# Last two experts' downs at the end of the load order, first two experts gathered as one pair, one stream of modulation weights later in the order: one layer of a GLA, MLA and MoE block on one core

## The chip, the core and the metric

One Trainium2 chip, one of its cores. The metric is the device time of one execution of the kernel in microseconds (us), as a median over runs. The core has five engines that run side by side, each with its own instruction stream: TensorE (PE in the profile, its weight loads PEld), VectorE (DVE), ScalarE (ACT), GpSimd (POOL) and SyncE (SP), which here only issues DMA transfers. PEq, DVEq, ACTq and SPq are the parts of these engines that handle branches, waits and issues.

## What is computed

One layer over 256 tokens of width 1024. A mixer (gated linear attention beside latent attention, merged and projected) is added to the stream, then a MoE of 32 experts with four of them per token. Both are modulated by six vectors that come from one product of the conditioning with `w_mod`, 1024 x 6144. The MoE, cut to its core:

```python
def _moe(h, p):
    logits = (tok @ p["router_w"] + p["router_b"]).astype(jnp.float32)
    top_v, top_i = lax.top_k(logits, TOP_K)                  # 4 of 32
    wts = jax.nn.softmax(top_v, axis=-1)
    combine = jnp.sum(jax.nn.one_hot(top_i, N_EXPERTS) * wts[..., None], axis=1)
    for e in range(N_EXPERTS):
        gate = jnp.minimum(tok @ p["w_gate"][e] + p["b_gate"][e], SWIGLU_LIMIT)
        up = jnp.clip(tok @ p["w_up"][e] + p["b_up"][e], -SWIGLU_LIMIT, SWIGLU_LIMIT)
        act = (up + 1.0) * gate * jax.nn.sigmoid(SWIGLU_ALPHA * gate)
        out = out + combine[:, e:e + 1] * (act @ p["w_down"][e] + p["b_down"][e])
```

Each of an expert's three matrices is 1024 x 1024 in 32-bit floats. The result is x + gt_f * rmsnorm(out), over the last axis.

## The kernel before

**Before the experts.** In the first 300 us the kernel computes the modulation vectors, the mixer and the router. Its instructions stand in an order written out by hand (`tc.manual_schedule`), on every engine. Two strands of work are interleaved there: the projection of the hidden states by `w_in` (the products `p_gate<-h0h,wsl` and their like, fed by `split`, in which ACT rounds a block of weights to `wsh`, L370, and DVE takes the remainder `wsl`, L371; a call `Q(n)` puts the next n steps of it into the order) and the linear attention (`scores` gives the masked product `at` on DVE, L988; `inner` and `outer` sum `po` on TensorE; `normed_o` gives `on` on DVE, L1016; `outputs` turns it). The weights of modulation stream `g` come in four loads of 2 MB, g0 to g3, through two buffers; DVE adds each up in four instructions, two pairs of 128 x 1024 (L325). A string such as `"g2:0"` given to `Q` puts one pair there; `ring.done("g2")` behind the second pair frees the buffer, into which g3 is loaded.

**The expert weights.** They go through a ring of ten tiles of 2 MB (class `Ring`): an expert takes six, two each of w_gate, w_up and w_down, in this order. SyncE issues their loads (L76), in the order of the list `src`; the load into a tile is issued once the tile's last reader is done and `ring.done(n)` has stood in the program, n tiles at a time. The last up and the last down are cut into four pieces a tile; the last down is cut by columns (`w_down_last`), so that its left half of the output can be finished before its right half is loaded.

**One expert.** `select` (DVE, tensors `G`) marks the rows, up to 64, that are routed to it; `gather` multiplies them out of `x1` on TensorE (`p_xg`, two groups, g = 0 and 1) for a pair of experts at a time (EB = 2), and DVE and ACT modulate the outcome to `X` (L1344, L1367). `gather_one` does the same for one expert, with rows and columns the other way round and a turning (`p_xT`) behind; it is used for experts 0 and 1. `project` runs gate and up (`p_gate`, `p_up`; a first product with `selb` adds the bias), 32 passes each; `turn` turns the 64 rows of `u` to `aT`; `down` gives `p_y`, 32 passes; `halves` splits it into `yh` and `yl` (ACT and DVE); `scatter` adds these with S, which holds positions and weights (from `slot_tokens`, `p_st`), to `acc`, one expert later, ahead of the next down. So TensorE's order in expert e is: gate, up, a group of the gather for the next pair, `turn`, scatter of expert e-1, `p_st`, down.

**More than 64 rows.** `trips` holds, for each expert, a count that says whether another 32 rows are needed. The engines read it (`blocks`: `TENSOR_LOAD trips`, L1582) and branch: a body under `tc.If(rv > 0)` repeats gate, up and down for these rows. In this input it is entered in expert 0 and in one other. Expert 0 has such a branch behind each half of each matrix; experts 1 to 9 behind the gate (L1660), behind the up (L1666) and behind the down (L1726); experts 10 to 30 behind the up, with both projections in one body, and behind the down; expert 31 behind each half of the down (L1733). A branch with freed tiles behind it is followed by a new load of the count on SyncE, which stands behind the issue of the loads (`freed`).

**The end.** Behind expert 31, `acc` is squared and summed by columns (ACT, L1763, `jf`), normed, multiplied and added to `x1`, and stored.

The releases of expert 1 and later, as they stand:

```python
            if early:
                with tc.If(rv > 0):
                    X1, S1, g1 = more_first()
                rv = freed(2)
```

## Time and profile before

| | before |
|---|---|
| median of three runs | 1265.72 us (1265.17 to 1267.21) |
| the profiled execution | 1266.84 us |
| its span, first to last instruction | 1265.1 us |
| mean granted TensorE clock | 0.984 |
| TensorE busy | 1148.6 us (91%) |
| VectorE, ScalarE, GpSimd busy | 405.5, 246.6, 79.6 us |
| moved by DMA | 463.51 MB, 366 GB/s over the span |

A share of busy time is a mean over stages with different limits: in the first 300 us the DMA moves 104 to 364 GB/s a slice, and from 380 us on, but for one slice of 329 and the last, 410 to 428. The times of single instructions come from the profiled execution, so they add up to its span and not to the median; it lies 1.1 us above the median. Between the span and its time there are 1.7 us.

### The profile page before, as it was taken

The page shows a single profiled execution, that of the slowest core. Times are in us where ns is not written, and L with a number is a line of the kernel's source. Part 1 is how long each engine was busy: PE and PEld are TensorE (multiplying, and loading weights), DVE is VectorE, ACT ScalarE, POOL GpSimd, SP SyncE. Part 2 cuts the span into 40 slices and gives each one's busy share as a digit, 9 for nine tenths or more (in the row PEclk, how much of TensorE's full clock was granted, in tenths as well). Part 3 has the DMA queues.
Part 4 walks back from the last instruction along what each step waited for, and adds up shares of the span by engine and source line. Part 5 has one row for each costly group of instructions (what it writes and reads, how often), then busy time and mean ns, then how long its engine had stood idle before and what let it go on. Part 6 is the DMA issues. An engine that isn't in the chain of part 4 may idle for free. (4 is left out here: it accounts for less than half of the span.)

```text
span 1265.1 us, 16274 instructions
## 1 busy us (share of the span) xinstructions
PE 1148.6 (91%) x6484; PEld 603.1 (48%) x6487; DVE 405.5 (32%) x787; ACT 246.6 (19%) x432; POOL 79.6 (6%) x62
## 2 busy tenths in 40 slices
PE   8999989999999999999998899999879879999884
PEld 5776778885344444444443344444333333444321
DVE  5667676665321212212121222221111211122112
ACT  4566443452210010101010011010100100101001
POOL 2346001300000000000000000000000000000000
PEclk9999998999999999999999999999989999999998
DMA  9842545885789999999999999999799999999993
GB/s 364 328 180 104 225 179 219 338 338 235 306 352 410 425 424 426 425 427 425 425 427 426 425 428 426 425 425 427 329 413 427 425 426 426 426 427 425 426 413 127
DMA packets 38053, 463.51 MB, mean 366 GB/s; under 512 B 4600, under 2 KB 4856, under 8 KB 10400
## 3 DMA queue, kind: packets, MB, share of 16 engines
q1 hardware_dynamic: 37488, 461.42, 87.6%
q8 instruction: 100, 1.64, 0.5%
q14 instruction: 33, 0.27, 0.1%
q10 hardware_dynamic: 432, 0.18, 0.1%
HBM read 460.53 MB, written 1.05 MB: 365 GB/s over the span
## 5 line engine op out<-in xcount | busy, mean ns | idle before, releaser
L204 PE MATMUL p_up<-w,X 128*64 128x512 f32 x1024 | 229.4, 594 | 13.5 <-DMA w<-in_w_up_dram 11.2
L204 PE MATMUL p_y<-w,aT 128*64 128x512 f32 (+1 forms) x1088 | 236.4, 599 | 1.0 <-ACT aT L1482 1.0
L204 PE MATMUL p_gate<-w,X 128*64 128x512 f32 x1024 | 231.8, 601 | 3.1 <-DMA w<-in_w_gate_dram 2.7
L204 PEld LDWEIGHTS p_up<-w,X 128*64 128x64 f32 x1024 | 87.9, 137 | 140.1 <-issue 110.5
L204 PEld LDWEIGHTS p_gate<-w,X 128*64 128x64 f32 x1024 | 94.6, 138 | 117.0 <-issue 112.5
L204 PEld LDWEIGHTS p_y<-w,aT 128*64 128x64 f32 (+1 forms) x1088 | 72.5, 136 | 144.2 <-issue 140.7
L1505 DVE TENSOR_TENSOR yl<-p_y,yh 128x512 fp32r<-128x512 f32 x33 | 22.8, 691 | 227.9 <-ACT yh L1504 221.1
L1449 DVE TENSOR_SCALAR g<-p_gate 128x512 f32<-128x512 f32 x32 | 22.1, 692 | 221.1 <-PE p_gate L204 212.8
L204 PE MATMUL p_xg<-G,x 128*128 128x128 f32 x480 | 63.1, 284 | 24.1 <-PEq L1666 21.5
L204 PEld LDWEIGHTS p_xg<-G,x 128*128 128x128 f32 x480 | 57.5, 195 | 49.1 <-issue 49.0
L1482 ACT COPY aT<-p_aT 128x512 f32<-128x512 f32 (+1 forms) x34 | 19.5, 574 | 304.8 <-PE p_aT L1480 304.8
L1454 DVE TENSOR_SCALAR u<-p_up 128x512 f32<-128x512 f32 x32 | 22.1, 691 | 173.0 <-PE p_up L204 173.0
L1450 ACT ACTIVATE s<-g 128x512 f32<-128x512 f32 (+1 forms) x34 | 21.0, 618 | 281.7 <-DVE g L1449 281.6
L214 POOL TENSOR_TENSOR rx<-rx,cst 128x1 f32<-128x1 f32 x2 | 1.5, 767 | 961.0 <-DVE rx L213 961.0
L1504 ACT CAST yh<-p_y 128x512 fp32r<-128x512 f32 x33 | 19.3, 585 | 212.7 <-PEq L1726 192.8
L204 PEld LDWEIGHTS <-selb 128*64 128x64 bf16 (+2 forms) x178 | 15.8, 104 | 83.5 <-issue 81.6
L204 PE MATMUL p_gate<-h0h,wsh 128*128 128x256 f32 x160 | 47.6, 297 | 0.0
L204 PE MATMUL p_gate<-h0h,wsl 128*128 128x256 f32 x160 | 46.0, 288 | 0.9 <-DVE wsl L371 0.9
L204 PE MATMUL p_gate<-h0l,wsh 128*128 128x256 f32 x160 | 45.5, 285 | 0.0
L1344 DVE TENSOR_SCALAR X<-p_xg,mA_gpref,mB_gpref 128x128 f32<-128x128 f32 x60 | 24.6, 410 | 63.3 <-PE p_xg L204 44.0
L371 DVE TENSOR_TENSOR wsl<-p,wsh 128x1024 fp32r<-128x1024 f32 x27 | 36.1, 1335 | 13.1 <-ACT wsh L370 13.0
L204 PE MATMUL p_gate<-RB,selb 128*64 128x512 bf16 x64 | 14.3, 403 | 26.3 <-PEq L1726 15.6
(430 smaller groups left out, 1417.6 us busy)
## 6 DMA issues: line engine op xcount, KB each, us to landing
w<-in_w_gate_dram SPq DMA_DIRECT2D x64, 2048.0 KB, 33.0
w<-in_w_up_dram SPq DMA_DIRECT2D x62, 2048.0 KB, 32.5
w<-in_w_down_dram SPq DMA_DIRECT2D x62, 2048.0 KB, 27.2
p<-in_w_in_dram SPq DMA_DIRECT2D x7, 2048.0 KB, 9.3
a<-in_w_mod_a_dram SPq DMA_DIRECT2D x8, 1024.0 KB, 9.6
f<-in_w_mod_f_dram SPq DMA_DIRECT2D x4, 2048.0 KB, 8.7
g<-in_w_mod_g_dram SPq DMA_DIRECT2D x4, 2048.0 KB, 7.8
wo<-in_w_out_dram SPq DMA_DIRECT2D x2, 2048.0 KB, 15.3
```

The lines of the kernel that those rows point to most:

```text
L204: nc.tensor.matmul(o, l, r, start=start, stop=stop)
L214: nc.gpsimd.tensor_tensor(dst, dst, C("nhalf")[:, :dst.shape[1]], op=ALU.pow)
L371: (eng or nc.vector).tensor_sub(lo, src, hi.bitcast(F32))
L1344: nc.vector.tensor_scalar(X[:, j], p[:, k], fA[:, 0, j:j + 1], fB[:, 0, j:j + 1], op0=ALU.mult, op1=ALU.add)
L1449: nc.vector.tensor_scalar(g, pg, LIMIT, None, op0=ALU.min)
L1450: nc.scalar.activation(s, g, AF.Sigmoid, scale=ALPHA)
L1454: nc.vector.tensor_scalar(u, pu, LIMIT, -LIMIT, op0=ALU.min, op1=ALU.max)
L1482: nc.scalar.copy(aT, p)
L1504: nc.scalar.copy(hi, p)
L1505: nc.vector.tensor_sub(lo, p, hi.bitcast(F32))
```

## The change

Five edits, all in the order of the program; the arithmetic of the result and the bytes that are moved stay as they are, but for the last w_up, which comes in two pieces in place of eight.

1. The two pairs of g2 move from `scores` of the second half (`"g2:0"`, `"g2:1"`) 13 and 17 DVE instructions back, and `ring.done("g2")` with them.
2. Experts 0 and 1 are gathered as a pair, as all others: `gather_one` is gone, and G of both is selected at the start. The pair of experts 2 and 3 then has its first group in expert 0 and its second in expert 1.
3. In expert 0 the count is read at its first branch, behind four blocks of w_gate, and no longer ahead of all of them.
4. Experts 1 to 3 (`SINGLE = 4`) free gate and up tile by tile, with a branch behind each half, as in expert 0.
5. In the list of loads the downs of experts 30 and 31 come last, behind the gate and up of both; the loops follow: expert 31's gate, up and `turn` run ahead of expert 30's down, and at the end stand the down of 30, the left half of the down of 31, the scatter of 30, the right half, and the scatter of both halves. Experts 30 and 31 have, as 1 to 9, a branch behind the gate and one behind the up; expert 31 has one in place of two in its down. `u` and `aT` of the last expert get room of their own in a buffer that is free (`RB`).

And in the loop for crowded experts, which this input doesn't enter, loads are issued by ScalarE and not SyncE.

```diff
+SINGLE = 4
...
-    for e in range(NE):
-        for n in ("w_gate", "w_up", "w_down"):
-            for c in range(2):
-                if e == NE - 1 and n == "w_down":
-                    w = a["w_down_last"][c]
-                    src.append(((8, 512), [(w[:, ts(q, 2)], ts(q, 2)) for q in range(4)]))
-                elif e == NE - 1 and n == "w_up":
-                    shape, w = rows_of(a[n][e, c])
-                    src.append((shape, [(w[:, ds(q, 1)], ds(q, 1)) for q in range(4)]))
-                else:
-                    src.append(rows_of(a[n][e, c]))
+    pairs = [(e, n) for e in range(NE - 2) for n in ("w_gate", "w_up", "w_down")]
+    pairs += [(e, n) for e in (NE - 2, NE - 1) for n in ("w_gate", "w_up")] + [(e, "w_down") for e in (NE - 2, NE - 1)]
+    for e, n in pairs:
+        for c in range(2):
+            if (e, n) == (NE - 1, "w_down"):
+                w = a["w_down_last"][c]
+                src.append(((8, 512), [(w[:, ts(q, 2)], ts(q, 2)) for q in range(4)]))
+            else:
+                src.append(rows_of(a[n][e, c]))
...
-    Q(1, "g2:0")
+    Q(1)
     norm(0)
     scores(1, 0)
-    Q(1, "g2:1")
+    Q(1)
...
-    Q(1)
+    Q(1, "g2:0")
     normed_o(1)
     Q(1)
     outputs(1)
     nc.vector.tensor_scalar(ltb, C("revbc"), 16.0, None, op0=ALU.mult)
     nc.vector.memset(oneb, 1.0)
     nc.vector.tensor_copy(sel, C("sel"))
-    Q(1, pool=2)
+    Q(1, "g2:1", pool=2)
     ring.done("g2")
...
-    select(G, 0, 0)
+    for i in range(EB):
+        select(G, i, i)
     more = more_gather(SLOTS, posm[:, :, 0:1])
     next(more)
-    first = gather_one(X, G, 0)
-    next(first)
+    gather(X, G, 0)
+    gather(X, G, 1)
     next(more)
-    next(first)
     next(more)
-    next(first)
...
-        Ws = [ring.take() for _ in range(6)]
+        Ws = [ring.take() for _ in range(6 if e < NE - 2 else 4)]
...
-        rv = blocks(e, None if e else loaded.ins)
+        rv = blocks(e) if e else None
...
-            project(0, p, of, X, 0, W, SLOTS, range(0, 4))
+            project(0, p, of, X, 0, W, SLOTS, range(0, 2))
             X1 = list(more)[-1]
+            project(0, p, of, X, 0, W, SLOTS, range(2, 4))
             softmax(0, 1)
             softmax(1, 1)
             nc.vector.tensor_copy(comb4.rearrange("p t (c e) -> p t c e", c=4),
                                   comb.unsqueeze(2).to_broadcast([128, 2, 4, 32]))
-            select(G, 1, 1)
-            project(0, p, of, X, 0, W, SLOTS, range(4, 6))
             chain.__exit__(None, None, None)
             ctx.enter_context(tc.manual_schedule(engines={E.PE}))
             p1 = more_bank(0, "g")
+            rv = blocks(e, loaded.ins)
             with tc.If(rv > 0):
                 project(0, p1, of, X1, 0, W, MORE, range(0, 4))
             rv = freed(1)
-            project(0, p, of, X, 0, W, SLOTS, range(6, 8))
+            project(0, p, of, X, 0, W, SLOTS, range(4, 8))
...
+            early = e < EARLY or e >= NE - 2
+            single = e < SINGLE
 
             def more_first():
                 X1 = list(more_gather(SLOTS, posm[:, :, e:e + 1]))[-1]
-                S1, w1 = slot_tokens(of, more_sid, "1")
-                return X1, S1, more_in(0, of, X1, W, w1)
-
-            if early:
+                return X1, *slot_tokens(of, more_sid, "1")
+
+            if single:
+                for k in range(2):
+                    if k:
+                        p = bankb("p_up", tag="g")
+                    p1 = more_bank(k)
+                    for half in range(2):
+                        js = range(4 * half, 4 * half + 4)
+                        project(k, p, of, X, SLOTS * i, W, SLOTS, js)
+                        if half:
+                            upped(p, g, u) if k else gated(p, g, toks[e][1])
+                        with tc.If(rv > 0):
+                            if k + half == 0:
+                                X1, S1, w1 = more_first()
+                            project(k, p1, of, X1, 0, W, MORE, js)
+                            if half and k:
+                                u1 = more_upped(p1, g1)
+                            elif half:
+                                g1 = more_gated(p1, w1)
+                        rv = freed(1)
...
-        if e and following[0] < NE:
-            if i == 0 or e == 1:
+        if following[0] < NE:
+            if i == 0:
                 Gn, Xn = block_tiles()
                 for k, f in enumerate(following):
                     select(Gn, k, f)
                 gather(Xn, Gn, 0)
             if i == 1:
                 gather(Xn, Gn, 1)
-        if e == 0:
-            nxt = gather_one(X, G, 1)
-            next(nxt)
-            next(nxt)
-        aT = turn(u, SLOTS)
-        if e:
+        aT = turn(u, SLOTS, aT=aT_last if e == NE - 1 else None)
+        if e == NE - 1:
+            pass
+        elif e:
             scatter(*todo)
-        else:
-            next(nxt)
...
+    e = NE - 2
+    S, S1, aT, u1, rv = ends[e]
+    Ws = [None] * 4 + [ring.take() for _ in range(2)]
+    todo = S, halves(down(aT, lambda k: Ws[4 + k // 4][:, k % 4], bankb("p_y", tag="g")))
+    with tc.If(rv > 0):
+        a1T = turn(u1, MORE, "1")
+        more_out(S1, [down_parts(a1T, lambda k: w_of(e, k, n), MORE, bankb(f"p_y1{n}")) for n in range(2)])
+    ring.done(2)
+    e = NE - 1
+    rv = blocks(e, ring.last.ins)
+    S, S1, aT, u1, _ = ends[e]
+    Ws = [None] * 4 + [ring.take() for _ in range(2)]
+    p = down_parts(aT, lambda k: w_of(e, k, 0), SLOTS, bankb("p_y0", tag="g"))
+    with tc.If(rv > 0):
+        a1T = turn(u1, MORE, "1")
+        more_out(S1, [down_parts(a1T, lambda k: w_of(e, k, n), MORE, bankb(f"p_y1{n}")) for n in range(2)])
+    scatter(*todo)
+    ys = halves(p)
+    p = down_parts(aT, lambda k: w_of(e, k, 1), SLOTS, bankb("p_y1", tag="g"))
+    scatter_parts(S, ys, 0, True)
+    scatter_parts(S, halves(p), 1, True)
```

Three places in the order of the instructions, as the compiled programs have it. A number behind a name tells buffers apart; an "x2" at the end is two in a row of the same form.

**DVE, behind the first half of the linear attention.** `sums<-g_1708` are the pairs of g2, `wsl` the remainders for the projection, `at`, `on` and `ro` the attention's. Before:

```order
L371 TENSOR_TENSOR wsl<-p_1344,wsh 128x1024
L325 SCALAR_TENSOR_TENSOR sums<-g_1708,cz,sums 128x1024 x2
L213 TENSOR_SCALAR ro_1766<-so_1765 128x4
L988 SCALAR_TENSOR_TENSOR at_1777<-p_at_1775,place_81 128x256
L988 SCALAR_TENSOR_TENSOR at_1781<-p_at_1779,place_81 128x256
L371 TENSOR_TENSOR wsl<-p_1620,wsh 128x1024
L325 SCALAR_TENSOR_TENSOR sums<-g_1708,cz,sums 128x1024 x2
L1016 TENSOR_TENSOR on_1767<-po_1626,ro_1766 128x512
L988 SCALAR_TENSOR_TENSOR at_1821<-p_at_1819,place_81 128x256
L988 SCALAR_TENSOR_TENSOR at_1825<-p_at_1823,place_81 128x256
L371 TENSOR_TENSOR wsl<-p_1620,wsh 128x1024
```

The change, first the same place and then the new one of g2:

```order
L370 TENSOR_TENSOR wsl<-p_1344,wsh 128x1024
L212 TENSOR_SCALAR ro_1764<-so_1763 128x4
L987 SCALAR_TENSOR_TENSOR at_1775<-p_at_1773,place_81 128x256
L987 SCALAR_TENSOR_TENSOR at_1779<-p_at_1777,place_81 128x256
...
L212 TENSOR_SCALAR ro_1913<-so_1912 128x4
L370 TENSOR_TENSOR wsl<-p_1620,wsh 128x1024
L324 SCALAR_TENSOR_TENSOR sums<-g_1708,cz,sums 128x1024 x2
L1015 TENSOR_TENSOR on_1914<-po_1772,ro_1913 128x512
L370 TENSOR_TENSOR wsl<-p_1824,wsh 128x1024
...
L370 TENSOR_TENSOR wsl<-p_1824,wsh 128x1024
L324 SCALAR_TENSOR_TENSOR sums<-g_1708,cz,sums 128x1024 x2
L370 TENSOR_TENSOR wsl<-p_1824,wsh 128x1024
```

The first pair has moved back over 13 instructions (`ro`, `at`, `wsl`, `on`, `o` and `ogl`), the second over 17, and the first one now stands directly ahead of the second `on`.

**TensorE, where the experts start.** `x_2294` and G give expert 0's rows, `p_xg` with 32x256 is the gather of its extra rows, `w_2199` and `w_2273` are its two w_gate tiles. Before:

```order
L204 MATMUL p_xg<-x_2294,G 64x512 x4
L204 MATMUL p_xg<-x_2294,G 32x256 x8
L1361 MATMUL p_xT_2891<-cst,xg 128x128 x2
L1361 MATMUL p_xT_2898<-cst,xg 128x128 x2
...
L1582 TENSOR_LOAD trips
L204 MATMUL p_gate<-RB,selb 64x512
...
L204 MATMUL p_gate<-w_2199,X 64x512 x8
L1426 MATMUL p_xT<-cst,xg 128x128 x2
L204 MATMUL p_gate<-w_2273,X 64x512 x4
L1625 COMPARE_AND_BRANCH
```

The change:

```order
L203 MATMUL p_xg<-G,x_2294 128x128 x16
L203 MATMUL p_xg<-x_2294,G 32x256 x8
...
L203 MATMUL p_gate<-RB,selb 64x512
...
L203 MATMUL p_gate<-w_2199,X 64x512 x4
L1397 MATMUL p_xT<-cst,xg 128x128 x2
L203 MATMUL p_gate<-w_2199,X 64x512 x4
L1554 TENSOR_LOAD trips
L1602 COMPARE_AND_BRANCH
```

The gather has 16 products of 128x128 in place of 4 of 64x512 (the trace shows two or more passes for one product), the two turnings behind it are gone, no product with w_2273 is left ahead of the branch, and the load of the count has moved from ahead of `p_gate` to directly ahead of its branch.

**TensorE, at the end.** `w_12187` and `w_12192` are the halves of the last down before, `w_12190` and `w_12195` in the change; `RB` is where the last `aT` now lies. Before:

```order
L204 MATMUL p_y_12465<-w_12187,aT 64x512 x8
L1733 COMPARE_AND_BRANCH
...
L1733 UNCONDITIONAL_BRANCH x2
L204 MATMUL acc_2811<-yh,S 128x512
...
L204 MATMUL acc_2813<-yl,S 128x512
L204 MATMUL p_y_12505<-w_12192,aT 64x512 x8
L1733 COMPARE_AND_BRANCH
...
L1733 UNCONDITIONAL_BRANCH x2
L204 MATMUL acc_2812<-yh,S 128x512
L204 MATMUL acc_2814<-yl,S 128x512
```

The change:

```order
L1554 TENSOR_LOAD trips
L203 MATMUL p_y_12591<-w_12190,RB 64x512 x8
L1744 COMPARE_AND_BRANCH
...
L1744 UNCONDITIONAL_BRANCH x2
L203 MATMUL acc_2811<-yh,S 128x512
L203 MATMUL acc_2812<-yh,S 128x512
...
L203 MATMUL acc_2814<-yl,S 128x512
L203 MATMUL p_y_12652<-w_12195,RB 64x512 x8
L203 MATMUL acc_2811<-yh,S 128x512
...
L203 MATMUL acc_2813<-yl,S 128x512
L203 MATMUL acc_2812<-yh,S 128x512
L203 MATMUL acc_2814<-yl,S 128x512
```

The scatter of expert 30 (`acc_2811` to `acc_2814` with `yh` and `yl`, eight products) now stands between the two halves of the last down, the scatter of the left half (`acc_2811`, `acc_2813`) behind the right half's product and no longer ahead of it, and one branch is left in place of two. Before, expert 30's scatter stood ahead of the first of these rows.

## Rows read from the trace of the kernel before

**Rows 1.** Stretches: us, busy of PE, PEld, DVE, ACT, POOL (instructions), PEclk, DMA share, GB/s.

```profile
190.00:199.00 9.00, 6.79 (x26) 5.92 (x27) 6.89 (x11) 0.00 (x0) 1.01 (x1) 0.50 0.15 62
304.00:316.00 12.00, 10.83 (x70) 4.38 (x71) 4.12 (x18) 0.57 (x2) 0.00 (x0) 0.86 0.04 10
381.00:1217.00 836.00, 764.09 (x3924) 335.39 (x3922) 167.89 (x354) 77.58 (x148) 0.00 (x0) 0.99 1.00 422
1243.00:1244.00 1.00, 1.00 (x6) 0.34 (x6) 0.00 (x0) 0.00 (x0) 0.00 (x0) 0.55 0.16 66
```

**Rows 2.** SyncE in order of time: start, us, line, operation, out<-in, count.

```profile
314.99 4.59 SPq L76 DMA_DIRECT2D w<-in_w_down_dram  x2
...
379.46 0.87 SPq L76 DMA_DIRECT2D w<-in_w_up_dram  x2
```

**Rows 3.** DVE in order of time; in brackets idle time before and its releaser.

```profile
187.66 2.48 DVE L325 SCALAR_TENSOR_TENSOR sums<-g,cz,sums 128x1024 f32<-128x1024 f32 x2 [4.93 <-DMA g<-in_w_mod_g_dram]
```

**Rows 4.** TensorE in order of time, 176 to 196 us.

```profile
176.48 1.05 PE L204 MATMUL po<-place,at 128*128 128x128 f32 x8
...
190.60 2.08 PE L204 MATMUL po<-place,at 128*128 128x128 f32 x8 [4.41 <-DVE at L988]
...
195.15 1.19 PE L204 MATMUL p_at<-qx,e 128*128 128x256 f32 x2 [1.62 <-DVE on L1016]
```

**Rows 5.** DVE in order of time, 229 us.

```profile
229.12 2.48 DVE L325 SCALAR_TENSOR_TENSOR sums<-g,cz,sums 128x1024 f32<-128x1024 f32 x2
```

**Rows 6.** TensorE in order of time, 232 us.

```profile
232.78 0.38 PE L204 MATMUL p_gate<-h0h,wsl 128*128 128x256 f32 x1 [0.41 <-DVE wsl L371]
```

**Rows 7.** The page, part 6: DMA issues, KB each, median us from issue to landing.

```profile
g<-in_w_mod_g_dram SPq DMA_DIRECT2D x4, 2048.0 KB, 7.8
```

**Rows 8.** TensorE in order of time, expert 0.

```profile
299.22 2.94 PE L204 MATMUL p_xg<-x,G 128*64 128x512 f32 x24 [0.76 <-DVE G L1331]
...
305.17 0.66 PE L204 MATMUL p_gate<-RB,selb 128*64 128x512 bf16 x2 [2.02 <-DVE trips L1576]
305.51 5.22 PE L204 MATMUL p_gate<-w,X 128*64 128x512 f32 x16
...
321.00 3.60 PE L204 MATMUL p_up<-w,X 128*64 128x512 f32 x16
...
331.93 1.94 PE L204 MATMUL p_xg<-x,G 128*64 128x512 f32 x8
...
336.26 0.38 PE L204 MATMUL p_st<-where,selb 128*128 128x512 bf16 x1 [0.92 <-ACT X L1367]
```

**Rows 9.** TensorE in order of time, experts 1 and 2.

```profile
358.61 0.44 PE L204 MATMUL p_up<-RB,selb 128*64 128x512 bf16 x2 [0.53 <-PEq L1660]
...
366.62 3.81 PE L204 MATMUL p_xg<-G,x 128*128 128x128 f32 x32 [0.71 <-PEq L1666]
...
370.79 0.50 PE L204 MATMUL acc<-yh,S 64*128 64x512 f32 x2
...
371.92 0.39 PE L204 MATMUL p_st<-where,selb 128*128 128x512 bf16 x1
...
395.75 2.10 PE L204 MATMUL p_xg<-G,x 128*128 128x128 f32 x16 [0.71 <-PEq L1666]
```

**Rows 10.** TensorE in order of time, expert 31.

```profile
1240.72 1.08 PE L1480 MATMUL p_aT<-cst,u 128*128 128x128 f32 x4 [5.28 <-PEq L1666]
...
1249.81 3.65 PE L204 MATMUL p_y<-w,aT 128*64 128x512 f32 x16
```

**Rows 11.** ACT in order of time, 1249 to 1251 us.

```profile
1249.52 0.60 ACT L1763 ACTIVATE jf<-acc 128x512 f32<-128x512 f32 x1 [1.38 <-PE acc L204]
1250.01 0.19 ACT L1763 ACTIVATION_READ_ACCUMULATOR jf<-acc 128x1 f32 x1
```

**Rows 12.** Branches of L1660 on PE: count, min/median/max ns, first and last start.

```profile
L1660 PEldq COMPARE_BRANCH  x9: 208/345/421, 353.6 to 573.8; - x9
```

**Rows 13.** Branches of L1666 on PE, as above.

```profile
L1666 PEldq COMPARE_BRANCH  x32: 70/339/6196, 361.4 to 1234.4; - x32
```

93 lines of the change are left out of this document (35 added, 58 removed).

## The prediction, made before the changed kernel was run

> **What bounds the kernel now.** The first view is the table of stretches, for its last column, the rate of the DMA. From 381 to 1217 us it stands at 422 GB/s, the DMA's share at 1.00 [rows 1]; an expert is six tiles of 2.1 MB, 12.6 MB, so 29.9 us at that rate, and TensorE, busy 764 of these 836 us, is the faster of the two. So behind 381 the loads set the pace, and nothing done faster on an engine there brings the end nearer. What does is the moment from which the rate is full. Between 304 and 316 it is 10 GB/s [rows 1]: all ten tiles of the ring are full and the first is given back only when SyncE issues the load at 314.99; the last issue that finds the DMA idle is the one at 379.46, when expert 1's downs come free [rows 2]. That release stands in TensorE's order, and so do all of the 300 us before it. So the second view is TensorE's order of time up to there, read for idle time and its releaser: each us that it loses ahead of 379.46 is a us of the end. The third is the end itself: the last weights land about 1244.4 us (in 1243 to 1244 there are still 66 GB/s [rows 1]; the rest is for the signal), while the span runs to 1265.1. These 20.7 us are work that the last bytes release.
>
> **The second stream of mod weights, g2.** DVE waits 4.93 us for g2 to land and then runs it in two pairs of 2.48 us [rows 3]; the attention mask product `at` stands behind it on DVE, and TensorE waits 4.41 us for that and 1.62 us more for `on` [rows 4]. Behind this idle time the granted clock is 0.50 (1.2 GHz) for the whole stretch 190 to 199, in which TensorE is busy 6.79 us [rows 1]; that the same eight `po` take 2.08 there and 1.05 before [rows 4] says that half of it, 3.4 us, is the clock's. With the pairs moved behind, g2 has landed long before DVE comes to it (187.6 against about 200), and all three go: 4.4 + 1.6 + 3.4 = 9.4. What they cost in the new place the trace does not show. The lower bound is 0; the upper is both pairs in full, 4.96. The nearest row is the pair of g3 at 229.12 [rows 5], of the same shape and in the same run of `wsl` splits: TensorE waited 0.41 us for the split behind it [rows 6]. I take that twice and 0.3 for `on`, which now stands right behind the first pair and which the turning of the outputs waits for: 1.1. Queued behind the moved pairs is also the load of g3, since its buffer comes free with the second: it is issued some 10 us later in the order than before, and lands 7.8 us behind that [rows 7], some 2 us before DVE's pair at 229.12 wants it; if it were late, DVE would stall there as it does now at 187. Net **8.2 us** (4.4 to 9.4).
>
> **The first experts.** Four terms up to the release at 379.46.
> - Start. TensorE begins to gather at 299.22 and to project at 305.17, after 2.02 us of waiting for the counts, `trips` [rows 8]. Now it waits for four `G` (0.76 us for two [rows 8], so some 0.3 more), gathers both experts (32 passes, 3.8 us as at 366.62 [rows 9]) and the extra rows (a third of the 2.94 at 299.22), and goes on at 304.35: 0.8. The counts come later in DVE's order, at some 307, but are now asked for behind four blocks of w_gate, at about 308.5, so that wait does not come back.
> - Clock. The 16 passes behind the wait took 5.22 us, 16 of the same form 3.60 [rows 8]; without the gap 1.6 goes (bounds 0 and 1.6).
> - Expert 0's tail. From `p_xg` at 331.93 to `p_st` at 336.26 there are 4.33 us, 0.92 of it a wait for ACT's last `X` [rows 8]. Now 16 passes of the next block's gather stand there (2.10, as at 395.75 [rows 9]) and the turning of `aT`, 0.6, with perhaps 0.3 of waiting for its copy: 1.35 less. Expert 1 then gathers one group and not two: 3.81 becomes 2.10 [rows 9], 1.7 less.
> - Against this, two more branches in expert 1, at 0.53 us each, as at 358.61 [rows 9]: 1.1 more. Experts 2 and 3 pay as much, but behind 379 that is TensorE's time and not the loads'.
>
> 0.8 + 1.6 + 1.35 + 1.7 - 1.1 = **4.4 us** (2 to 5.5) earlier for expert 1's downs. The releases one at a time send expert 1's gates off some 4 us sooner than in a pair, but the DMA then runs dry anyhow until the downs are free, which still come in a pair: that edit is worth nothing in the end while the downs are last. What SyncE has to do meanwhile (up to twelve loads of counts in a row, before the issue that is last) fits in the 12 us of expert 1's down.
>
> **The end.** Loads: the last up goes in two pieces and not eight; I cost it at 0.4 us (0 to 1). Now TensorE stands idle 5.28 us at a branch of expert 31, behind which `aT`, the scatter of expert 30 and both halves of the last down (3.65 each) queue up [rows 10]: all of that runs when the weights have landed. In the new order expert 31 is gated, upped and turned while 8 MB are still to come. Counted back from the last landing, T: the last 4.2 MB take 10 us, so the second half of expert 30's down starts at T-10; it takes 3.65, a branch 0.53, the first half of the last down 3.65, a branch 0.53, expert 30's scatter 1.1 (370.79 to 371.92 [rows 9]), the second half 3.65: 13.1, so it ends at T+3.1, TensorE's own pace and not the last byte's. Before, it ended at 1253.46 and the span 11.64 later. To these 11.64 us comes what lay under the second half of the down and no longer does: ACT now squares `acc` of the left half (0.60 and 0.19 [rows 11]) ahead of the last `yh`, and waits for that `acc`, 0.55: 1.35. The end is T+16.1, against 1265.1 - 1244.4 = 20.7 before: **4.6 us** (0 to 8).
>
> The crowded loop's loads move to ACT's queue. The loop isn't entered, and SyncE waits there for the same nine semaphores as before: 0.
>
> **Sum.** 8.2 + 4.4 + 0.4 + 4.6 = 17.6. The profiled execution took 1266.84 us (span 1265.1), 1.1 above the median of 1265.72. 1266.84 - 17.6 = 1249.2, and by the median 1248.1: **1248**.
>
> **The branches, by row and by rule.** The new order has six more of them in experts 1 to 3 and four shorter ones in 30 and 31. A branch that is not taken costs TensorE 0.2 to 0.42 us over the short bodies of L1660, but at L1666, whose body from expert 10 on holds both projections, up to 6.2 [rows 12, 13]. The Trainium skill (Runtime: NRT & Kernel Launch, "Instruction fetch mechanics") says that a branch to a target outside the window of instructions at hand has to wait until that page is fetched, and so advises against control flow. By that rule long bodies pay and short ones don't, and the rows agree; halving the bodies of experts 30 and 31 would take away the 5.28 us that the sum has already.
>
> **Rivals.**
> 1. *DVE is short where g2 now stands* (or g3 comes late behind it). For: the splits there wait on ACT and DVE in turn, and even g3's pair cost 0.41. Against: it cost no more. Both pairs paid in full: 3.9 less, 1252.
> 2. *The end is not shortened.* TensorE comes to expert 30 late: the branches of experts 2 and 3 leave it 2 us behind the loads, and a 6 us branch at expert 28 or 29 would do the rest. For: its slack is only 72 in 836 us. Against: it waits for weights already. Without the 4.6: 1253.
> 3. *More than reckoned*: the pairs cost nothing, the last down ends with the last byte (2 to 3 us less): 1242.
> 4. *Slower: the new branches pay the page fetch.* If each of the six in experts 1 to 3 cost 6.2 and not 0.53, expert 1's downs would be 11.3 later than reckoned and expert 3's, which then become the last to find the DMA idle, some 34 less the slack of 2 that they have: 1280. From 3.3 such branches on the gain is gone. Against: 9 experts have run with bodies of that length, none over 0.42 [rows 12].
>
> **How the numbers follow.** Forecast as summed (1244 to 1251) 0.60; rival 1 0.15, rival 2 0.13, rival 3 0.09, rival 4 0.03. The range takes the forecast with the bounds of its unknown terms, rivals 1 and 2, and part of 3: 1241 to 1256. A measurement of this kernel tells 0.2%, 2.5 us, from no change: faster by more 0.96, within 0.01, slower 0.03.
>
> **What would show it.** On DVE no wait for g, and TensorE without idle time and at clock 1.00 between 186 and 200; a `p_gate` wait of under 1 us where the pairs now stand; the first expert's projection some 9 us earlier than 305.17 and with no wait for `trips`; SyncE's issue behind expert 1's downs at 366 to 368 in place of 379.46, and the full rate, 422 GB/s or more, from there; no branch over 1 us in experts 30 and 31, the last traffic at about 1231 and 16 us from there to the end. It is wrong if the first full-rate stretch does not begin earlier by the sum of the first two terms, or if the distance from the last byte to the end stays near 21.

## The result, and the profile after

The changed kernel takes 1249.9 us in the median of four runs (1249.61 to 1250.3), the kernel before in the same runs 1266.47 (1265.17 to 1268.71): a ratio of 0.9872, with a 95% interval of 0.9859 to 0.9885, or 16.6 us less. The forecast was 1248, 17.6 less, with a range of 1241 to 1256.

The page of the changed kernel, parts 1 (busy time) and 2 (slices of the span):

```profile
PE 1143.7 (92%) x6491; PEld 605.2 (48%) x6495; DVE 403.5 (32%) x781; ACT 244.7 (20%) x426; POOL 79.6 (6%) x62
...
PEclk9999999999999999999999999999989999999998
...
GB/s 365 336 163 116 209 173 255 390 345 264 314 343 423 424 426 426 426 426 424 426 427 425 427 426 426 425 426 425 347 400 426 425 427 425 426 427 426 425 424 187
```

TensorE is busy 1143.7 us, 4.9 less than before; the slices at full rate begin with the thirteenth, with one of 347 and the last below.

Stretches of the changed kernel, columns as in [rows 1]:

```profile
190.00:199.00 9.00, 9.00 (x93) 8.71 (x92) 2.97 (x5) 4.24 (x12) 1.01 (x1) 1.00 0.70 269
304.00:316.00 12.00, 10.85 (x88) 3.98 (x88) 5.81 (x14) 3.98 (x5) 0.00 (x0) 1.00 0.92 345
370.00:1206.00 836.00, 766.71 (x3928) 340.23 (x3926) 167.84 (x354) 77.58 (x148) 0.00 (x0) 0.99 1.00 422
1231.00:1232.00 1.00, 1.00 (x9) 0.59 (x9) 0.00 (x0) 0.13 (x1) 0.00 (x0) 1.00 0.33 131
1232.00:1233.00 1.00, 1.00 (x8) 0.43 (x8) 0.52 (x1) 0.45 (x1) 0.00 (x0) 1.00 0.02 8
```

The lower clock and the idle time at 190 to 199 are gone (9.00 us busy of 9, clock 1.00; before 6.79 and 0.50). Between 304 and 316 the DMA moves 345 GB/s and not 10, and a stretch of 836 us that begins 11 us earlier than the one in [rows 1] moves 422 GB/s as that one does. The last traffic stands in 1232 to 1233 (8 GB/s), before in 1243 to 1244. SyncE's issue behind expert 1's downs stands at 368.51, before at 379.46 [rows 2]:

```profile
368.51 0.96 SPq L77 DMA_DIRECT2D w<-in_w_up_dram  x2
```

**Where to measure from.** Single executions of one order differ by up to 2.5 us ahead of any edit. One row of TensorE that lies ahead of every edit, with a wait of 0.57 us for `st`, begins at 162.99 before, at 163.21 in the changed kernel, and in a second profile of the changed kernel (c_after) at 164.97; here it is called the common row. These are the rows of the two profiles of the changed kernel:

```profile
163.21 0.65 PE L203 MATMUL p_ds<-place,place 64*64 64x128 f32 x12 [0.57 <-DVE st L957]
```

```profile
164.97 0.65 PE L203 MATMUL p_ds<-place,place 64*64 64x128 f32 x12 [0.57 <-DVE st L957]
```

Counted from this row the two agree to 0.05 us: expert 1's downs are free at 205.31 and 205.33, the span ends at 1085.30 and 1085.32. So all differences below are counted from it. The end goes by the span as the page gives it, to 0.1 us, and only the changed kernel has a second profile: a difference of some tenths between two other kernels rests on one execution of each. The table has, for each kernel's profile, the start of this row, and from there the issue behind expert 1's downs, the landing of the last weights and the end of the span; the last column is end less landing. Medians in it come from different chips and calls, on which the kernel before took 1266.5 to 1269.1 us.

| kernel | median us (runs) | row at | issue | last landing | end | end - landing |
|---|---|---|---|---|---|---|
| before | 1266.47 (4) | 162.99 | 216.47 | 1081.44 | 1102.11 | 20.67 |
| changed | 1249.90 (4) | 163.21 | 205.31 | 1069.55 | 1085.30 | 15.75 |
| c_after: changed, again | 1251.06 (4) | 164.97 | 205.33 | 1069.50 | 1085.32 | 15.82 |
| x1: g2 back | 1259.01 (6) | 164.85 | 212.91 | 1077.41 | 1093.25 | 15.84 |
| x2: no single releases | 1249.28 (4) | 163.26 | 203.64 | 1068.06 | 1083.84 | 15.78 |
| x3: old end | 1251.39 (4) | 163.59 | 205.35 | 1069.85 | 1086.21 | 16.36 |
| x4: count first | 1254.11 (4) | 163.61 | 208.77 | 1072.78 | 1088.59 | 15.81 |
| x5: single gathers | 1252.66 (4) | 163.52 | 206.77 | 1071.08 | 1086.87 | 15.79 |
| x7: g2 one step earlier | 1250.52 (4) | 163.29 | 203.68 | 1068.02 | 1083.91 | 15.89 |
| y1: before, code shifted | 1263.88 (12) | 163.19 | 216.71 | 1081.14 | 1099.31 | 18.17 |
| y3: x2 and x3 | 1250.78 (4) | 165.54 | 203.67 | 1068.43 | 1084.16 | 15.73 |
| w1: y3, long jump | 1257.49 (4) | 163.54 | 203.59 | 1069.17 | 1090.56 | 21.39 |
| w2: x2, long jump | 1253.50 (4) | 165.15 | 203.73 | 1068.61 | 1085.05 | 16.44 |
| z1: x2, x7 and a shorter end | 1246.68 (4) | 163.93 | 202.38 | 1067.03 | 1081.88 | 14.85 |

The change brings 16.8 us by the last but one column: 11.2 at the issue, 11.9 at the last landing, and 4.9 behind it.

**The first experts.** TensorE of the changed kernel, to be set beside [rows 8, 9]:

```profile
292.41 3.81 PE L203 MATMUL p_xg<-G,x 128*128 128x128 f32 x32 [1.20 <-DVE G L1330]
...
297.37 0.41 PE L203 MATMUL p_gate<-RB,selb 128*64 128x512 bf16 x2
...
311.73 3.60 PE L203 MATMUL p_up<-w,X 128*64 128x512 f32 x16
...
322.66 2.05 PE L203 MATMUL p_xg<-G,x 128*128 128x128 f32 x16
...
325.82 3.65 PE L203 MATMUL p_y<-w,aT 128*64 128x512 f32 x16 [0.68 <-ACT aT L1455]
...
348.68 0.43 PE L203 MATMUL p_up<-RB,selb 128*64 128x512 bf16 x2 [0.52 <-PEq L1644]
...
357.46 2.02 PE L203 MATMUL p_xg<-G,x 128*128 128x128 f32 x16 [0.70 <-PEq L1644]
...
361.29 7.09 PE L203 MATMUL p_y<-w,aT 128*64 128x512 f32 x32
```

The gather starts 6.8 us earlier than in [rows 8], the first gate product 7.8 and the up of expert 0 9.3; its down (325.82; before at 336.56, by the same view) 10.7. Expert 1's two more branches then cost some of it (348.68 against 358.61: 9.9; 357.46 against 366.62: 9.2), and the shorter gather gives it back: expert 1's down starts at 361.29 and before at 372.24, 10.95 earlier.

**The end.** TensorE of the changed kernel, beside [rows 10]:

```profile
1218.15 0.63 PE L1452 MATMUL p_aT<-cst,u 128*128 128x128 f32 x4 [1.61 <-DVEq L1735]
...
1222.70 3.65 PE L203 MATMUL p_y<-w,aT 128*64 128x512 f32 x16 [0.34 <-DMA w<-in_w_down_dram]
1227.07 3.65 PE L203 MATMUL p_y<-w,RB 128*64 128x512 f32 x16 [0.71 <-ACTq L1744]
1230.87 0.50 PE L203 MATMUL acc<-yh,S 64*128 64x512 f32 x2 [0.15 <-PEq L1744]
...
1232.00 3.65 PE L203 MATMUL p_y<-w,RB 128*64 128x512 f32 x16
```

Up to the right half's product no idle time is over 1.61 us; the down of 30, the two halves of the last one and the scatter between them follow with gaps of 0.34 us (for weights), 0.71 and 0.15 (at a branch). The branch of expert 31 behind its up is short now and takes 0.21 us by the trace, where in the kernel before it took 6.0.

### The profile page after: what moved, and what is told of

Its sections match the earlier page's. It is cut to its first block, busy times and chain, and to the rows that moved or that the text cites. A ratio compares the mean times of both kernels' runs of the same rounds, so it can differ in the third digit from the quotient of the medians.

```text
span 1248.5 us, 16384 instructions
## 1 busy us (share of the span) xinstructions
PE 1143.7 (92%) x6491; PEld 605.2 (48%) x6495; DVE 403.5 (32%) x781; ACT 244.7 (20%) x426; POOL 79.6 (6%) x62
## 5 line engine op out<-in xcount | busy, mean ns | idle before, releaser
L203 PE MATMUL p_y<-w,aT 128*64 128x512 f32 (+1 forms) x1056 | 228.9, 598 | 2.0 <-ACT aT L1455 1.7
L203 PE MATMUL p_xg<-G,x 128*128 128x128 f32 x512 | 68.0, 288 | 24.6 <-PEq L1664 19.5
L203 PEld LDWEIGHTS p_xg<-G,x 128*128 128x128 f32 x512 | 62.5, 199 | 49.5 <-issue 49.5
L328 POOL TENSOR_TENSOR sums<-sums,f 128x1024 f32<-128x1024 f32 x14 | 35.8, 2588 | 33.6 <-ACT f L326 22.2
```

The lines of the kernel that those rows point to most:

```text
L203: nc.tensor.matmul(o, l, r, start=start, stop=stop)
L328: nc.gpsimd.tensor_add(to, to, v)
```

## The experiments

**One edit undone at a time.** x1 puts g2 back:

```diff
     queries(1)
-    Q(1)
+    Q(1, "g2:0")
     norm(0)
     scores(1, 0)
-    Q(1)
+    Q(1, "g2:1")
...
     norm(1)
-    Q(1, "g2:0")
+    Q(1)
     normed_o(1)
...
-    Q(1, "g2:1", pool=2)
+    Q(1, pool=2)
```

> The changed kernel with the two pairs of g2 back in their old place in the order. Theory, from the two traces: up to the first gather of expert 0 the change has gained 6.8 us and up to the loads of expert 1's downs 10.95; what g2 costs in its old place is 7.3 of that (TensorE waits 4.4 and 1.6 there and runs 3.4 us longer at the lower clock, less some 2 us that the new place costs), and all of it reaches the end: 1249.9 + 7.3 = 1257.2 us (1256 to 1258.2). Prediction's size: 8.2, 1258.1. Rival: the ring's first loads or the waits behind take up a part of it, so that the end moves by less than 5: below 1255.

Measured: 1259.01 us; from the common row the issue comes 7.6 us later and the end 7.95. So all of it reaches the end. The waits for `at` and `on` (4.45 and 1.62 us) and the lower clock (0.68 in 186 to 200) are back at the same places. TensorE of x1:

```profile
192.44 2.07 PE L203 MATMUL po<-place,at 128*128 128x128 f32 x8 [4.45 <-DVE at L987]
```

In the changed kernel the pairs stand here on DVE, and TensorE then waits for the `wsl` behind the second:

```profile
200.01 2.48 DVE L324 SCALAR_TENSOR_TENSOR sums<-g,cz,sums 128x1024 f32<-128x1024 f32 x2
...
207.96 4.28 DVE L324 SCALAR_TENSOR_TENSOR sums<-g,cz,sums 128x1024 f32<-128x1024 f32 x2
```

```profile
213.43 0.39 PE L203 MATMUL p_gate<-h0h,wsl 128*128 128x256 f32 x1 [1.44 <-DVE wsl L370]
```

The second pair takes 4.28 us and not 2.48, beside two additions on GpSimd (its spans are rough):

```profile
207.43 1.63 POOL L861 TENSOR_TENSOR sums<-sums,RB 64x512 f32<-64x512 f32 x1 [10.72 <-ACT RB L859]
209.79 1.38 POOL L865 TENSOR_TENSOR RB<-sums,RB 32x512 bf16<-32x512 f32 x1 [0.73 <-ACT RB L863]
```

x4 reads the count ahead of the first gate product again:

```diff
-        rv = blocks(e) if e else None
+        rv = blocks(e, None if e else loaded.ins)
...
-            rv = blocks(e, loaded.ins)
             with tc.If(rv > 0):
                 project(0, p1, of, X1, 0, W, MORE, range(0, 4))
```

> The changed kernel with the count of expert 0 read ahead of its first gate product again. The count is written at 299.2 us, TensorE is ready for the product at 297.4, so it waits some 2.1 us. Theory: behind the wait the clock is granted at half for some passes again, as before (16 passes in 5.22 and not 3.60 us): 2.1 + 1.6 = 3.7, 1253.6 us. Rival: the gap alone, at full clock: 1252.0 us. Rival: the first experts' pace doesn't reach the end: 1249.9.

Measured: 1254.11 us, 3.3 more from the common row. TensorE waits 2.05 us, and the eight passes behind the wait take 3.32 us where they took 1.88:

```profile
299.82 0.67 PE L203 MATMUL p_gate<-RB,selb 128*64 128x512 bf16 x2 [2.05 <-DVE trips L1548]
300.20 3.32 PE L203 MATMUL p_gate<-w,X 128*64 128x512 f32 x8
```

The stretch 299 to 303 has a clock of 0.57, in the changed kernel 1.00:

```profile
299.00:303.00 4.00, 3.18 (x10) 1.16 (x9) 0.46 (x4) 0.00 (x0) 0.00 (x0) 0.57 0.00 0
```

2.05 + 1.44 = 3.5 at the issue (3.46 measured). The first theory holds: this gap costs its own length and then the clock. Not every gap does: behind waits of 1.20 (292.41), 1.44 (213.43) and 1.61 us (1218.15) the changed kernel's clock is 1.00.

x5 gathers experts 0 and 1 one by one again (`gather_one` and its four steps as in the kernel before; the count stays at its branch):

```diff
-    for i in range(EB):
-        select(G, i, i)
+    select(G, 0, 0)
...
-    gather(X, G, 0)
-    gather(X, G, 1)
+    first = gather_one(X, G, 0)
...
-        if following[0] < NE:
-            if i == 0:
+        if e and following[0] < NE:
+            if i == 0 or e == 1:
```

> The changed kernel with experts 0 and 1 gathered one by one again, the count still read at its branch. Theory, from the two traces: the start gets 1.4 us shorter (one gather of 8 passes less, a shorter wait for G), expert 0's tail 1.45 and expert 1's gather 1.78 longer: the load behind expert 1's downs is issued at 370.3 us and not 368.5, and the run takes 1.8 us longer, 1251.7 us. Rival: the pace of the first experts is set by the loads of expert 1's weights, and nothing changes.

Measured: 1252.66 us, 1.6 more from the common row, 1.5 at the issue. TensorE:

```profile
292.31 2.94 PE L203 MATMUL p_xg<-x,G 128*64 128x512 f32 x24 [0.76 <-DVE G L1330]
...
296.16 0.41 PE L203 MATMUL p_gate<-RB,selb 128*64 128x512 bf16 x2
...
325.54 0.38 PE L203 MATMUL p_st<-where,selb 128*128 128x512 bf16 x1 [0.91 <-ACT X L1366]
...
357.45 3.81 PE L203 MATMUL p_xg<-G,x 128*128 128x128 f32 x32 [0.71 <-PEq L1671]
...
363.08 7.09 PE L203 MATMUL p_y<-w,aT 128*64 128x512 f32 x32
```

Here the gate starts 3.85 us behind the gather's start (4.96 in the changed kernel), `p_st` waits 0.91 for ACT's `X`, and expert 1's gather takes 3.81 in place of 2.02. The pair is worth 1.6 by itself: less than its two savings, since it costs at the start.

x2 frees gate and up of experts 1 to 3 in pairs:

```diff
-SINGLE = 4
+SINGLE = 1
```

> The changed kernel with experts 1 to 3 freeing gate and up in pairs, with one branch behind each matrix, as experts 4 to 9 do. Theory of the prediction: the single releases are worth nothing at the end, because the load behind expert 1's downs still starts the full rate, and they cost TensorE two branches and two breaks, 1.5 us by the two traces, so without them that load is issued at 367.0 and not 368.5 and the run takes 1248.4 us. Rival: the loads issued one by one at 344 to 357 us keep the DMA busy where pairs would leave it idle (265 to 272 GB/s at that place before), and their bytes are wanted at the end: 1251 to 1254 us.

Measured: 1249.28 us on a chip on which the kernel before took 1267.74; from the common row the issue comes 1.67 us and the end 1.46 us earlier:

```profile
366.90 0.82 SPq L77 DMA_DIRECT2D w<-in_w_up_dram  x2
```

So the single releases cost 1.5 us and give nothing back; the theory of the prediction holds.

x3 puts the whole end back: the loads' order, the pieces of the last up, expert 31's loop, branches and scatters.

```diff
-    pairs = [(e, n) for e in range(NE - 2) for n in ("w_gate", "w_up", "w_down")]
...
+    for e in range(NE):
+        for n in ("w_gate", "w_up", "w_down"):
...
-            early = e < EARLY or e >= NE - 2
+            early = e < EARLY
...
-            ends[e] = S, S1, aT, u1, rv
+            for n in range(2):
+                ys = halves(down_parts(aT, lambda k: w_of(e, k, n), SLOTS, bankb(f"p_y{n}", tag="g")))
...
```

> The changed kernel with the old end: downs of experts 30 and 31 in the old order of the loads, last up in eight pieces, expert 31's loop, branches and scatters as before. Theory: from the last landing to the end 20.7 us in place of 15.75, and 0.4 for the pieces: 1249.9 + 5.4 = 1255.3 us (1254.5 to 1256.5). Rival: the end of the changed kernel is short because TensorE came to it early by what was gained at the start, not by the order; then it stays within 1 us of 1249.9.

Measured: 1251.39 us, 0.9 more from the common row: 0.3 at the last landing, 0.6 behind it. That is near the rival's size and not the theory's. The row that matters is TensorE's wait at expert 31's branch, 1.60 us here and 5.28 in [rows 10], with the same code around it; the branch itself takes 0.34 us by the trace, before 6.03:

```profile
1226.83 0.63 PE L1454 MATMUL p_aT<-cst,u 128*128 128x128 f32 x4 [1.60 <-DVEq L1728]
```

**Why the old end was long in one kernel and short in the other.** The kernel before has a stall at this branch, and x3 has none. Its code lies 62 instructions further on in TensorE's program, mostly through the branches that were added in experts 1 to 3. y1 shifts the code of the kernel before by the same 62, by instructions in a body that isn't entered:

```diff
                 with tc.If(rv > 0):
+                    if e == 5:
+                        pad = more_bank(0)
+                        mm(pad[:MORE], of.to_broadcast([128, MORE]), RB[:, 0, :256], True, False)
+                        for _ in range(15):
+                            mm(pad[:MORE], X[:, 0, ds(0, MORE)], W(0, 0)[:, :256], False, False)
                     X1, S1, g1 = more_first()
```

> The kernel before, with 62 more TensorE instructions in the body of expert 5's first branch, which this input doesn't enter: no executed instruction is added, but all code behind it lies 62 instructions further on, exactly where it lies in the kernel x3 (the changed kernel with the old end). Theory: which of the long branches stall for 6 us is decided by where they lie in the program, so they stall where x3's do, and expert 31's (at 1234 us before) no longer does: from the last landing to the end 16.4 us in place of 20.7, and the run some 4.3 us under the kernel before, 1262 us. Rival: the stall of expert 31 belongs to the old order of the end (few instructions left, loads still landing), and stays: 1266.5 us, as before.

Measured: 1263.88 us in 12 runs (1261.07 to 1267.35), a ratio of 0.9972 (0.9960 to 0.9984); from the common row 2.8 less than before. TensorE at the branches of experts 30 and 31:

```profile
1210.99 1.09 PE L1480 MATMUL p_aT<-cst,u 128*128 128x128 f32 x4 [2.85 <-PEq L1671]
...
1239.55 0.63 PE L1480 MATMUL p_aT<-cst,u 128*128 128x128 f32 x4 [1.60 <-DVEq L1738]
```

The stall of expert 31 is gone (1.60), though no executed instruction was added or taken away. But expert 30 now waits 2.85 us at its branch, which takes 6.1 us by the trace (0.35 in x3, though TensorE is idle there too, for 2.50 us and with no releaser in the profile), and the passes behind run slower (`aT` 1.09 us for 0.60). 18.2 us are left behind the last landing, not 16.4; that this branch is why is argued and not shown. Half of the theory holds: position has a say. That all stalls of y1 would be those of x3 doesn't.

The traces say more of it. Among the branches over long bodies, from expert 10 on, those that took over 0.9 us are the same nine in the changed kernel, c_after, x1, x3, x4, x5 and x7: experts 10, 12, 15, 17, 20, 22, 24, 27 and 29. y1 shares eight of them (that of 17 took 0.67 us) and adds expert 30. The kernel before has 12, 17, 19, 21, 24, 26, 29 and 31. x2 and z1, without the single releases, have 12, 17, 21, 24, 27 and 29, and so have y3, w1 and w2 (below), each with one to two more. So which branches are slow repeats from one execution to the next and changes with the code ahead of them.

y3 is x3 without the single releases, which brings the code to within 14 instructions of its place in the kernel before.

```diff
-SINGLE = 4
+SINGLE = 1
```

> The changed kernel with the old end, as x3, and without the single releases in experts 1 to 3, as x2: its branches from expert 10 on lie 14 instructions further on than in the kernel before, and not 62 as in x3. Theory: as in the kernel before expert 31's branch stalls for some 6 us, and the distance from the last landing to the end is 20.7 us: 1254 us, 4 more than the changed kernel, where x3 lost 1.5. Rival: x3's 1.5 is what the end's order is worth; with x2's gain of 1.4: 1250 us.

Measured: 1250.78 us; 15.73 us behind the last landing, and a wait of 1.74 us at the branch:

```profile
1226.77 0.63 PE L1454 MATMUL p_aT<-cst,u 128*128 128x128 f32 x4 [1.74 <-PEq L1666]
```

By the trace this branch takes 2.50 us (0.34 in x3, 6.03 before), and TensorE waits only 0.14 us more than in x3. The theory fails here: the old end, at nearly the old place, has no stall of 6 us. But its place is 14 instructions off the old one, so the place isn't ruled out by this. So the next two force the stall. w1 is y3 and w2 is x2 with 600 more instructions in the body of expert 31's branch behind its up, so that the jump is long:

```diff
             with tc.If(rv > 0):
+                    if e == NE - 1:
+                        pad = more_bank(1)
+                        mm(pad[:MORE], of.to_broadcast([128, MORE]), RB[:, 0, :256], True, False)
+                        for _ in range(150):
+                            mm(pad[:MORE], X[:, 0, ds(0, MORE)], W(0, 0)[:, :256], False, False)
```

> The kernel y3 (old end, no single releases) with some 600 more TensorE instructions in the body of expert 31's branch behind its up, which isn't entered; so the branch jumps over some 900 instructions and not 314. Theory: the new order of the end is worth next to nothing by itself, and what the kernel before lost there was the stall of this branch (5.28 us of idle time in place of 1.7, and the slower clock behind it, together 4.9 us). So with a jump as far as that, which must stall, the distance from the last landing to the end is 20.6 us and the run 4.9 us longer than y3: 1255.7 us. Rival: the old end takes T+16 whatever the branch does: 1250.8 us.

> The kernel x2 (new end, no single releases) with the same 600 instructions in the body of expert 31's branch behind its up. Prediction's story of the end: expert 31 is gated, upped and turned while 8 MB are still to land, so a stall there is hidden: 15.8 us from the last landing to the end, 1249.5 us. Theory now: TensorE has no slack there (it waits only 0.34 us for weights behind that branch), so a stall of 5.3 in place of 1.6 us moves the end by 3.3: 19 us from the last landing, 1252.8 us.

Measured: w1 1257.49 us, w2 1253.50. From the common row w1 ends 6.4 us behind y3 (4.9 was expected; 5.7 of it lie behind the last landing, 0.7 ahead of it), w2 1.2 behind x2; behind the last landing there are 21.39 and 16.44 us. The medians show less of a difference: w1 is 6.7 us over y3 and w2 4.2 over x2, with the kernel before 2.4 and 1.3 us slower on this chip than on theirs, and 4.0 us lie between w1 and w2, on one chip and in one call. TensorE of w1, and its branches of that line (count, min/median/max ns, first and last start):

```profile
1215.98 6.35 PE L205 MATMUL p_up<-w,X 128*64 128x512 f32 x28
1222.53 1.08 PE L205 MATMUL p_up<-w,X 128*64 128x512 f32 x4 [0.20 <-DMA w<-in_w_up_dram]
1228.87 1.09 PE L1454 MATMUL p_aT<-cst,u 128*128 128x128 f32 x4 [5.26 <-PEq L1666]
```

```profile
L1666 PEldq COMPARE_BRANCH  x32: 70/337/6567, 350.9 to 1222.5; - x32
```

And of w2:

```profile
1210.63 7.09 PE L203 MATMUL p_up<-w,X 128*64 128x512 f32 x32
1220.32 0.63 PE L1452 MATMUL p_aT<-cst,u 128*128 128x128 f32 x4 [2.60 <-PEq L1664]
```

```profile
L1664 PEldq COMPARE_BRANCH  x32: 70/335/6422, 352.6 to 1213.8; - x32
```

The last branch of the line, expert 31's, takes 6.0 us in both by the trace; it starts at 1222.5 in w1 and at 1213.8 in w2. In w1 TensorE has just got the last piece of the up weights (its last four passes start at 1222.53), so the stall begins when there is hardly anything left to run, 5.26 us of it are idle, and the passes behind run slower (`aT` 1.09 for 0.63). In w2 the up weights are all there: the branch is reached 3.9 us before the up's passes end (1210.63 + 7.09 = 1217.72), the stall runs beside them, and 2.60 us of idle time remain, of which 1.6 are there without a stall too. By the profile the theory of 19 us behind the last landing falls, and the prediction's reading, that the stall is hidden there, stands but for 0.7 us. The median of w2, 1253.50, is nearer to what that theory gave (1252.8) than to 1249.5; its profiled execution starts the common row 1.9 us later than x2's, and where the rest lies no profile shows.

**Two versions beyond.** x7 moves the pairs of g2 one step ahead each:

```diff
     outer(1)
-    Q(1)
+    Q(1, "g2:0")
     norm(1)
-    Q(1, "g2:0")
+    Q(1, "g2:1")
     normed_o(1)
...
-    Q(1, "g2:1", pool=2)
+    Q(1, pool=2)
```

> The changed kernel with the pairs of g2 each one step earlier: the first ahead of norm(1), where DVE waits 3.25 us for ScalarE's wsh, the second where the first now stands. Theory: the first pair lies in that wait, the second no longer runs beside GpSimd's two additions, which took it 4.28 us and not 2.48, and TensorE's wait of 1.44 us for the wsl behind it goes: 1248.4 us. Rival: the wait only moves to the new places: 1249.9.

> The changed kernel again, beside the three others of this call and on the same chip, so that their differences of a microsecond or two can be read: 1249.9 us.

Measured: x7 1250.52 us (1248.94 to 1250.61), c_after on the same chip 1251.06 (1249.58 to 1252.19): medians 0.5 apart, with ranges that overlap, so the times don't show the gain. From the common row, in one profile, x7 ends 1.4 earlier. DVE of x7:

```profile
195.02 2.47 DVE L324 SCALAR_TENSOR_TENSOR sums<-g,cz,sums 128x1024 f32<-128x1024 f32 x2
...
200.00 2.48 DVE L324 SCALAR_TENSOR_TENSOR sums<-g,cz,sums 128x1024 f32<-128x1024 f32 x2
...
208.27 1.86 DVE L370 TENSOR_TENSOR wsl<-p,wsh 128x1024 fp32r<-128x1024 f32 x1 [0.24 <-ACT wsh L369]
```

The pairs take 2.47 and 2.48 us, the first in the gap, and TensorE's longest wait between 164 and 224 us is 0.23. What stands beside GpSimd's additions now, a `wsl`, takes 1.86 in place of 1.2, and nobody waits for it.

z1 has x2's and x7's edits, and at the end the scatter of expert 30 behind the right half:

```diff
-    scatter(*todo)
-    ys = halves(p)
+    ys = halves(p, ("g", "s"))
     p = down_parts(aT, lambda k: w_of(e, k, 1), SLOTS, bankb("p_y1", tag="g"))
+    scatter(*todo)
     scatter_parts(S, ys, 0, True)
-    scatter_parts(S, halves(p), 1, True)
+    scatter_parts(S, halves(p, ("u", "aT")), 1, True)
```

> The changed kernel with what the runs so far point to: no single releases in experts 1 to 3 (1.4 us by x2), g2's pairs one step earlier (1.4 us by x7), and at the end the scatter of expert 30 behind the right half of the last down and ahead of the left half's scatter, in place of between the two halves, with buffers of their own for the two halves' splits: the right half starts 1.1 us earlier and the 0.85 us of waiting for its split lie under the scatters, 1.2 us. Together 4.0: 1245.9 us. Rival: the last weights land only 0.7 us behind the right half's start, so the end gains under 0.5: 1246.8 us.

Measured: 1246.68 us (1246.5 to 1247.52), the kernel before in the same runs 1269.08: a ratio of 0.9831 (0.9806 to 0.9856). From the common row it ends 3.4 us ahead of the changed kernel, 2.5 of it at the last landing and 0.9 behind it. Its end on TensorE, without a gap from the right half on:

```profile
1225.26 3.65 PE L203 MATMUL p_y<-w,RB 128*64 128x512 f32 x16 [0.71 <-ACTq L1744]
1229.21 3.65 PE L203 MATMUL p_y<-w,RB 128*64 128x512 f32 x16 [0.30 <-PEq L1744]
1232.80 0.50 PE L203 MATMUL acc<-yh,S 64*128 64x512 f32 x2
...
1234.96 0.39 PE L203 MATMUL acc<-u,S 128*128 128x512 f32 x1
```

The end's share lies between theory (1.2) and rival (under 0.5). z1 beats both kernels: by the trace clearly, by the ratios' intervals (up to 0.9856, and from 0.9859) just so. What each of its three edits adds no run tells apart.

## Why the prediction was right, step by step

- **What bounds.** Right: the end follows the issue behind expert 1's downs. What an undone edit ahead of it (x1, x2, x4, x5) did at that issue came out at the end within 0.4 us. It came at 368.51, forecast 366 to 368.
- **g2, 8.2 (4.4 to 9.4).** 7.95 at the end by x1, 7.6 at the issue. All three parts of its old cost are back when it is. The new place cost TensorE 1.44 us at one `wsl` and 0.23 at another, where twice 0.41 had been taken, and 0.12 for `on` in place of 0.3: 1.8 and not 1.1, and 9.4 - 1.8 is the 7.6 of x1. (By its own terms the step gave 9.4 - 1.1 = 8.3 and not 8.2.) What the step missed is GpSimd: the second pair stood beside two of its additions and took 4.28 us for 2.48, while beside g3's first pair, the nearest row that it took [rows 5], GpSimd rests. A nearer row stood in the trace of the kernel before, right where the second pair went: a `wsl` of 1.86 us, where others take 1.22, beside the first of these additions.

```profile
216.97 1.86 DVE L371 TENSOR_TENSOR wsl<-p,wsh 128x1024 fp32r<-128x1024 f32 x1 [0.23 <-ACT wsh L370]
```

```profile
216.13 1.63 POOL L862 TENSOR_TENSOR sums<-sums,RB 64x512 f32<-64x512 f32 x1 [9.80 <-ACT RB L860]
```

The Trainium skill (SBUF — State Buffer, "Who interferes with whom") says that an instruction of DVE with two inputs in SBUF and one of GpSimd that reads SBUF contend; the trace agrees, with 1.8 us more beside additions of 1.63 and 1.38. One step was wrong without effect: the line that frees g2's buffer did not move with the pairs, against what stands ahead of the prediction and in it; g3's load was issued 2.1 us later by the profiles (212.27, before 210.12) and not 10, right behind the second pair, and DVE did not wait for it (g3's first pair starts at 221.85).
- **The first experts, 4.4 (2 to 5.5).** 11.16 at the issue less x1's 7.6: 3.6. From the common row, by place: start 0.4 (0.8 forecast; the wait for four G was 1.20 us, where 0.76 + 0.3 had been taken), clock 1.5 (1.6), expert 0's tail 1.5 (1.35), expert 1's gather 1.8 (1.7), branches -1.6 (-1.1). The branches are the term that was mis-sized: besides two branches at 0.53 the gate and the up run in two pieces each; x2 has 1.67. That the single releases gain nothing while the downs come last was right; they cost 1.5 us by x2. The count's wait and its clock are worth 3.3 by x4, the pair of gathers 1.6 by x5.
- **The last up in fewer pieces, 0.4.** x3 lands its last byte 0.3 later.
- **The end, 4.6 (0 to 8).** 4.9, and its course as reckoned: TensorE at its own pace, the last product (1232.00 + 3.65) ends 2.9 us behind the last landing, 3.1 were forecast. But the term is the price of a stall and holds only against a kernel that has it: in x3 and y3 the old end takes 16.4 and 15.7 us, the new one 15.75, so against them the new end is worth 0.9 us in all (x3) and not 4.6. In the changed kernel the branch of expert 31 is short and doesn't stall at all (0.21 us): the 4.9 are for the most part a stall that is gone, not one that is hidden. The prediction named both ways, the order that hides it and the halved body, so its term holds for the two kernels that it was made for; that the stall can go away with a shift of the code alone, and the worth of the new order with it, it did not see. What the order hides is shown by one profile each of w1 and w2: with the stall in both, the old end takes 21.4 us and the new one 16.4 (4.0 us apart by the medians).
- **The branches.** None of the twelve at the halves of experts 1 to 3 took over 0.43 us, so rival 4 was rightly held small:

```profile
L1644 PEldq COMPARE_BRANCH  x12: 208/271/428, 340.1 to 411.0; - x12
```

The rule that the prediction drew from the Trainium skill (Runtime: NRT & Kernel Launch, "Instruction fetch mechanics") holds by length in the main: the long jumps of w1 and w2 take 6.0 us, the short ones under 0.5 in the changed kernel, and over all the profiles but for two (1.84 us in x5, 1.30 in w1). Which of the jumps of 314 instructions stall changes with the place of the code (y1 against before), and y1's expert 30, at the place of x3's and with a stall that x3 doesn't have, says not with that alone. What else decides it is open.
- **The sum.** At the issue 12.6 were forecast and 11.2 measured (g2 0.6 less, the first experts 0.8), at the last landing 13.0 and 11.9, at the end 17.6 and 16.8, by the medians 16.6. Rivals 1 to 3 stay out: g2's pairs cost neither 4.96 in their new place nor nothing, and the end got shorter. (Rival 3's terms, 1.1 and at most 3 us less, give 1244 and not 1242.)

## What to carry to other kernels

Where loads set the pace, find the issue from which they run full, and count each edit by what it does there: what four of them did there came out at the end within 0.4 us. A gap on TensorE can be paid twice, by its length and by the slower clock behind it, so a wait of 2.05 us was worth 3.3; waits of 1.20 to 1.61 us cost their length alone: read the clock behind each gap. To price an instruction in a new place, look for a row in that place, and at what the other engines do there. And before a gain is put down to an order of work, ask whether it removes a stall that a shift of the code removes too: put the order back, and force the stall in both.

## What the runs showed of the hardware that was not expected

- A stall at a branch of 314 instructions came and went with 62 instructions that are never executed (y1 against before: 5.28 us of idle TensorE to 1.60), and a branch that TensorE's sequencer reaches early, with its weights landed, stalls beside the passes still queued (w2: 6.0 us, 2.60 of it idle).
- DVE beside GpSimd: the pair of 128x1024 took 4.28 us in place of 2.48, a `wsl` 1.86 in place of 1.2 (in the kernel before too).
- Two executions of one program differed by 1.8 us ahead of the common row and by under 0.05 in the 1085 us behind it (changed and c_after). Whether that holds for the spread of other runs (y1: 1261.07 to 1267.35 us) isn't shown.
